# One large first load issued as three strided parts, ahead of the start barrier, in a kernel bound by data movement

## Chip, cores and metric

The kernel runs on one core of a Trainium2 chip. The metric is the time of one execution on the device in microseconds (us); lower is better. "The span" is the time from the first to the last instruction in a profile; it is 1.8 us shorter than the run's time.

## The reference

```python
def setup_inputs():
    batch, seq, dim = (32, 512, 2048)
    return {'x': np.random.randn(batch, seq, dim).astype(np.float32)}

def reference(x):
    half_dim = x.shape[-1] // 2
    x1, x2 = (x[..., :half_dim].copy(), x[..., half_dim:].copy())
    silu_x1 = x1 * (1 / (1 + np.exp(-x1)))
    return (silu_x1 * x2).astype(np.float32)
```

The input has 134.2 MB, the output 67.1 MB, and there is little arithmetic for each byte.

## The kernel before

Sixteen tiles of 1024 rows each; a partition holds 8 whole rows, 64 KB that lie together in memory. There are two input and two output buffers. ACT issues the loads and computes Silu in four chunks a tile, DVE multiplies, SP issues the stores.

```python
def issue_ahead_of_the_first_barrier(nc):
    head, body = nc.main_func.blocks[:2]
    load = next(ins for ins in body.instructions if type(ins).__name__ == "InstDMACopy")
    at = next(
        j for j, ins in enumerate(head.instructions)
        if ins.engine == load.engine and type(ins).__name__ == "InstDrain"
    )
    body.instructions = [ins for ins in body.instructions if ins.name != load.name]
    head.instructions = head.instructions[:at] + [load] + head.instructions[at:]
# ... (cut: sizes, pools, the plan of tiles)
    nc.at_finalize(issue_ahead_of_the_first_barrier)
    ctx.enter_context(tc.manual_schedule())
    loaded = {}

    def load(i):
        xt = in_pool.tile([P, K, in_cols], dt, name="xt")
        nc.scalar.dma_start(out=xt[:, :plan[i][1], :], in_=view(x_flat, i))
        loaded[i] = xt

    load(0)
    load(1)
    for i in range(n_tiles):
        # ... (cut)
        for c in range(0, k, KC):
            ce = min(c + KC, k)
            nc.scalar.activation(out=ot[:, c:ce, :], in_=xt[:, c:ce, :half],
                                 func=mybir.ActivationFunctionType.Silu)
            nc.vector.tensor_mul(out=ot[:, c:ce, :], in0=ot[:, c:ce, :],
                                 in1=xt[:, c:ce, half:])
            if last:
                nc.sync.dma_start(out=ov[:, c:ce, :], in_=ot[:, c:ce, :])
        if not last:
            nc.sync.dma_start(out=ov, in_=ot[:, :k, :])
        if i + 2 < n_tiles:
            load(i + 2)
```

The first load already stands ahead of the barrier with which the program starts, so that ACT's issue of it begins at 0.13 us of the span.

## Time and profile before

| | before |
|---|---|
| time, median of 3 runs | 470.96 us (470.91 to 471.08) |
| span of the profiled run | 468.9 us |
| busy: DVE, ACT | 30%, 25% |
| bytes moved | 201.35 MB, 429 GB/s on average |

The page of the kernel before: its span, the busy share of the engines, the busy tenths of the 16 DMA engines and the rate in 40 slices, and the chain of waits that ended last.

```profile
span 468.9 us, 269 instructions
DVE 142.3 (30%) x64; ACT 118.2 (25%) x65; POOL 0.2 (0%) x4
...
DMA  9899999999999998999999999999999989999998
GB/s 431 375 447 403 447 447 447 403 419 431 447 447 403 447 492 363 442 492 391 458 403 439 456 447 403 409 442 447 447 403 444 467 386 447 442 419 481 400 409 354
...
DMA 80%; DVE 15%; ACT 3%; DVEq 0%; issue 0%
```

The data movers hardly rest (the DMA row is 8 or 9 tenths in every slice); both compute engines idle most of the time (busy 30% and 25%). So in this kernel I expect a us in which the data movers do not move to come out as a us at the end.

The timeline of the kernel before, first 34 us: start, duration, engine (ACTq is ACT's sequencer, which issues DMAs), line, operation.

```profile
0.13 1.13 ACTq L74 DMA_DIRECT2D xt<-in_x_dram  x2
...
1.29 1.28 ACT L87 ACT_TABLE_LOAD   x1 [1.29 <-PEq L117]
21.88 7.31 ACT L87 ACTIVATE ot<-xt 128x2048 f32<-128x2048 f32 x4 [19.31 <-DMA xt<-in_x_dram]
23.82 8.90 DVE L92 TENSOR_TENSOR ot<-ot,xt 128x2048 f32<-128x2048 f32 x4 [23.82 <-ACT ot L87]
32.74 0.38 SPq L100 DMA_DIRECT2D out_dram<-ot  x1
32.75 0.35 ACTq L74 DMA_DIRECT2D xt<-in_x_dram  x1
```

ACT issues two loads, loads Silu's table while it waits, and starts on the first tile at 21.88 us. The first store is issued at 32.74 us.

The chain that ended last, in order of time (start, duration, what), beginning, second load and end:

```profile
0.92 43.60 DMA xt<-in_x_dram
...
55.41 47.19 DMA xt<-in_x_dram
...
404.13 46.88 DMA xt<-in_x_dram
...
451.03 1.92 ACT ot L87
```

The instructions on the input tile of the kernel before; the three numbers are the shortest, median and longest duration in ns of an issue on ACT.

```profile
L74 ACTq DMA_DIRECT2D xt<-in_x_dram x16: 334/366/376, 0.1 to 404.1; - x16
```

Below the page lie the records of single DMA packets. In this kernel one packet is one partition's row: 64 KB for a load, 32 KB for a store (8 KB for those of the last tile). The records do not name the engine; a figure "an engine" is a sum over all packets divided by 16. From them, with times from the start of the span:

```
kernel before                                     us
issue of the first load begins, ends              0.13, 0.50
first packets of the 16 engines begin             1.14 to 1.84, mean 1.32
first packets last                                2.47 to 3.44, on average 0.64 more than later ones
a load packet in mid-run lasts                    2.418   (27.1 GB/s an engine)
the load packet just ahead of an engine's first
store packet lasts                                3.18 to 3.42, on average 0.87 more than later ones
all load packets near the first store, longer by  0.90 an engine
last packet of all ends                           467.62
```

Each engine starts its next packet as the last one ends: between 5 and 450 us fewer than 16 of these packets are in flight for 1.0 us in all.

### The profile page before, as it was taken

To read this page: it belongs to the slowest core of one execution; us is meant where nothing else is said; L and a number is where in the kernel's file an instruction comes from. 1 tells how busy PE (TensorE), PEld (TensorE's weight loads), DVE (VectorE), ACT (ScalarE), POOL (GpSimd) and SP (SyncE) were. 2 spreads that over 40 slices of the span, in tenths; PEclk is the share of its full clock that TensorE was granted. 3 is DMA by queue.
4 is the path that set the end of the run, shared out by engine and by line. 5 is a ranking of instruction groups with operands and counts; after the bars stand their busy time and mean duration, and the time that the engine had idled before them with its cause. 6 is when DMAs were issued, how large, how long until landed. Compare 5 with 4: busy or idle time off the path is not lost.

```text
span 468.9 us, 269 instructions
## 1 busy us (share of the span) xinstructions
DVE 142.3 (30%) x64; ACT 118.2 (25%) x65; POOL 0.2 (0%) x4
## 2 busy tenths in 40 slices
DVE  0070705106061160601507025070250702407034
ACT  1142406023060330603206032060420604106051
POOL 0000000000000000000000000000000000000000
DMA  9899999999999998999999999999999989999998
GB/s 431 375 447 403 447 447 447 403 419 431 447 447 403 447 492 363 442 492 391 458 403 439 456 447 403 409 442 447 447 403 444 467 386 447 442 419 481 400 409 354
DMA packets 5042, 201.35 MB, mean 429 GB/s; under 512 B 560, under 2 KB 560, under 8 KB 560
## 3 DMA queue, kind: packets, MB, share of 16 engines
q10 hardware_dynamic: 2304, 134.22, 66.4%
q1 hardware_dynamic: 2736, 67.11, 33.2%
q14 instruction: 2, 0.02, 0.0%
HBM read 134.22 MB, written 67.11 MB: 429 GB/s over the span
## 4 chain that ended last, share of the span: by engine, by line
DMA 80%; DVE 15%; ACT 3%; DVEq 0%; issue 0%
DMA xt<-in_x_dram 80%; DVE ot L92 15%; ACT ot L87 3%; DVEq L128 0%
## 5 line engine op out<-in xcount | busy, mean ns | idle before, releaser
L92 DVE TENSOR_TENSOR ot<-ot,xt 128x2048 f32<-128x2048 f32 x64 | 142.3, 2286 | 319.5 <-ACT ot L87 319.5
L87 ACT ACTIVATE ot<-xt 128x2048 f32<-128x2048 f32 x64 | 116.9, 1897 | 338.8 <-DMA xt<-in_x_dram 338.8
L87 ACT ACT_TABLE_LOAD x1 | 1.3, 1283 | 1.3 <-PEq L117 1.3
L117 POOL MEMSET const-uint8-127<- 128x1 uint8 x1 | 0.1, 102 | 0.0
L117 POOL MEMSET const-bfloat16-1.0<- 128x1 bf16 x1 | 0.1, 101 | 0.0
L117 POOL MEMSET const-float32-0.0<- 128x1 f32 x1 | 0.1, 98 | 0.2 <-issue 0.2
L117 POOL MEMSET const-float32-1.0<- 128x1 f32 x1 | 0.1, 98 | 0.0
## 6 DMA issues: line engine op xcount, KB each, us to landing
out_dram<-ot SPq DMA_DIRECT2D x15, 4096.0 KB, 39.8
out_dram<-ot SPq DMA_DIRECT2D x4, 1024.0 KB, 5.7
xt<-in_x_dram ACTq DMA_DIRECT2D x16, 47.1
```

What stands on the lines that cost most here:

```text
L87: nc.scalar.activation(out=ot[:, c:ce, :], in_=xt[:, c:ce, :half], func=mybir.ActivationFunctionType.Silu,)
L92: nc.vector.tensor_mul(out=ot[:, c:ce, :], in0=ot[:, c:ce, :], in1=xt[:, c:ce, half:],)
L117: nc = _bacc.Bacc("TRN2", target_bir_lowering=False, num_devices=1)
```

## The change

The intent is that data starts to flow earlier after the issue of a first transfer with fewer rows. The first load is split into the partitions 0, 4, 8, ..., the ones halfway between (2, 6, 10, ...), and the odd ones, and all three parts are put ahead of the barrier.

```diff
-def issue_ahead_of_the_first_barrier(nc):
+def issue_ahead_of_the_first_barrier(nc, count):
     head, body = nc.main_func.blocks[:2]
-    load = next(ins for ins in body.instructions if type(ins).__name__ == "InstDMACopy")
+    loads = [ins for ins in body.instructions if type(ins).__name__ == "InstDMACopy"][:count]
     # ... (cut: all of `loads` are moved instead of one)
+    STARTING = [slice(0, None, 4), slice(2, None, 4), slice(1, None, 2)]
     # ... (cut)
-    nc.at_finalize(issue_ahead_of_the_first_barrier)
+    nc.at_finalize(lambda nc: issue_ahead_of_the_first_barrier(nc, len(STARTING)))
+    def load_parts(queue, dst, src, split):
+        for ps in STARTING if split else [slice(None)]:
+            queue.dma_start(out=dst[ps], in_=src[ps])
     def load(i):
         xt = in_pool.tile([P, K, in_cols], dt, name="xt")
-        nc.scalar.dma_start(out=xt[:, :plan[i][1], :], in_=view(x_flat, i))
+        load_parts(nc.scalar, xt, view(x_flat, i), split=i == 0)
     # ... (cut)
-            nc.sync.dma_start(out=ov, in_=ot[:, :k, :])
+            nc.sync.dma_start(out=ov, in_=ot)
```

The last line names the same region as before.

More of the change, by code (lines that the diff above doesn't have):

```diff
@@ L6 @@
 from concourse._compat import with_exitstack
-def issue_ahead_of_the_first_barrier(nc):
+def issue_ahead_of_the_first_barrier(nc, count):
     head, body = nc.main_func.blocks[:2]
-    load = next(ins for ins in body.instructions if type(ins).__name__ == "InstDMACopy")
+    loads = [ins for ins in body.instructions if type(ins).__name__ == "InstDMACopy"][:count]
     at = next(
         j for j, ins in enumerate(head.instructions)
-        if ins.engine == load.engine and type(ins).__name__ == "InstDrain"
+        if ins.engine == loads[0].engine and type(ins).__name__ == "InstDrain"
     )
-    body.instructions = [ins for ins in body.instructions if ins.name != load.name]
-    head.instructions = head.instructions[:at] + [load] + head.instructions[at:]
+    names = {ins.name for ins in loads}
+    body.instructions = [ins for ins in body.instructions if ins.name not in names]
+    head.instructions = head.instructions[:at] + loads + head.instructions[at:]
 @with_exitstack
```

## The prediction

> **What bounds the kernel.** Data movement, almost without a gap. The page's DMA row is 8 or 9 tenths in nearly every slice, mean 429 GB/s; DVE is busy 30%, ACT 25%. In the packet records a 64 KB load packet takes 2.418 us on its engine (27.1 GB/s), and each of 16 engines starts the next as the last ends. Every engine owes 128 load packets, 120 store packets of 32 KB (1.213 us) and 32 of 8 KB (0.309 us): 465 us. The first starts at 1.14 us of the span, the last ends at 467.6. What is not transfer is 1.3 us before the stream runs, some 0.6 us by which the first 16 packets are longer than later ones (2.5 to 3.4 us), and about 0.5 us at the end. The chain of waits agrees: 80% loads.
>
> **What the change does.** The first load, one issue of 128 rows of 64 KB, becomes issues of 32, 32 and 64 rows, all ahead of ACT's barrier drain. Bytes, row size, compute and its order stay (the store's changed slice is the same region).
>
> Added: two issues on ACT, 0.33 to 0.38 us each in the timeline. ACT's drain moves from 0.55 to about 1.2 us, the second load's issue from 0.92 to about 1.6 us. Neither is critical: the first part alone queues 4.8 us of work. Also 32 completion packets, two per engine at 9 ns: 0.02 us.
>
> Removed: some of the start. The issue runs from 0.13 to 0.50 us; engines begin between 1.14 and 1.39, two at 1.80 and 1.84. All finish their first packet together, at 4.24 to 4.60, whenever they began, as if data flowed only from about 1.85[...]. If a quarter as many descriptors make that sooner, the stream starts 0.1 to 0.5 us earlier and, saturated to its end, all of that comes off the time. If it is a first-access latency, nothing does. My estimate of the net: -0.3 us, 0.06%.
>
> **The risk.** [...] I give one in five to a loss of several us.
>
> **Predicted:** 470.7 us (before 470.96), range 470.0 to 473.0. Faster by over 2%: 0.01; within 2%: 0.86; slower by over 2%: 0.13.
>
> **What would show each step.** Timeline: three ACT issues, the last ending near 1.2 us; second load issued near 1.6. Packet records: earliest packet before 1.1 us, the first 16 closer together. The first ACTIVATE starts at 21.4 to 21.9 us (21.88 before); the last load lands 0.1 to 0.5 us before 451.0, as does the last store, 467.96. [...]
>
> **What would make it wrong.** [...] or engines idling between the parts.

The forecast's sum came to 470.96 - 0.3, about 470.7 us. The -0.3 is my estimate of the net: 0.1 to 0.5 us from an earlier start, or nothing, less 0.02 us for completion packets. The 4.8 us that the first part queues are an estimate too: two load packets of 2.418 us on each engine. The risk, that the strided parts of the first load would move more slowly: the one in five, the 0.13 for slower by over 2% and the upper part of the range, to 473.0 us, stood for it.

## The result

The changed kernel takes 471.94 us (median of 6 runs, 471.85 to 472.38) against 471.02 us (6 runs, 470.71 to 471.44): ratio 1.0021, 95% interval 1.0008 to 1.0033. By the 2% mark it is the same; the loss of about 0.9 us is nonetheless clear of the noise.

The page of the changed kernel, the same lines:

```profile
span 470.6 us, 274 instructions
...
DVE 142.4 (30%) x64; ACT 118.2 (25%) x65; POOL 0.2 (0%) x4
...
DMA  9999999999999999999999999999999999999997
GB/s 379 423 446 382 421 434 446 434 423 468 421 415 434 468 412 412 446 462 418 418 429 473 429 396 451 462 413 418 446 462 412 407 479 429 423 407 454 432 401 329
...
DMA 79%; DVE 15%; ACT 3%; DVEq 0%; issue 0%
```

At this grain nothing has changed: the bound is the same, and the page alone would not find 0.2%. The timeline does better. The changed kernel, first 36 us:

```profile
0.13 2.85 ACTq L76 DMA_DIRECT2D xt<-in_x_dram  x4
...
22.75 1.28 ACT L95 ACT_TABLE_LOAD   x1 [22.75 <-DMA xt<-in_x_dram]
24.05 7.31 ACT L95 ACTIVATE ot<-xt 128x2048 f32<-128x2048 f32 x4
25.99 8.90 DVE L100 TENSOR_TENSOR ot<-ot,xt 128x2048 f32<-128x2048 f32 x4 [25.99 <-ACT ot L95]
34.92 0.38 SPq L108 DMA_DIRECT2D out_dram<-ot  x1
34.92 0.35 ACTq L76 DMA_DIRECT2D xt<-in_x_dram  x1
```

Two things differ. The issues at the start last until 2.98 us (0.13 + 2.85) instead of 1.26. And the table load, 1.28 us, now comes after the load has landed: the first Silu waits for three transfers instead of one, and the trace has two of these waits on an extra instruction (a semaphore wait at 22.68 us) that stands ahead of the table load. So the first Silu starts 2.17 us later and the first store is issued 2.18 us later, though the load itself landed only 0.8 us later (22.66 against 21.86).

The chain, the same places:

```profile
2.64 43.34 DMA xt<-in_x_dram
...
56.87 47.10 DMA xt<-in_x_dram
...
405.53 47.09 DMA xt<-in_x_dram
...
452.64 1.92 ACT ot L95
```

The loss is there after the second load, which lands at 45.97 us instead of 44.52, and does not grow much afterwards: 1.45 us at the second load, 1.61 at the last. So what happens before 46 us is all there is to explain.

The issues on the input tile:

```profile
L76 ACTq DMA_DIRECT2D xt<-in_x_dram x18: 348/366/615, 0.1 to 405.5; - x18
```

The longest issue is 615 ns. The three strided ones last 0.550, 0.602 and 0.615 us; no load issue of the kernel before lasts over 0.376. And in the packet records, for this profile and for a second one of the same kernel (run "after_again" below):

```
                                          before  changed  changed again
first packet of any engine begins           1.14     1.47     1.46
first packets begin, mean                   1.32     1.75     1.60
first packets longer by, mean               0.64     0.58     0.68
load packets longer at the first store,
  us an engine                              0.90     1.50     1.50
engines on which such a packet starts
  before 37.5 us / long packets in all     16/16     4/20     7/23
second load: last engine done after first   0.38     2.30     2.16
last packet of all ends                   467.62   469.25   468.47
```

The sum for the first pair: 0.43 us from the later start, -0.06 from the first packets, 0.60 from the packets at the first store; that leaves 0.66 of the 1.63 us for what the slowest engine lags behind the mean more than it did before. For the second profile: 0.28 + 0.04 + 0.60 = 0.92 of 0.85, the lag being a little smaller than before. The start was in the prediction, with the wrong sign. The first store was not in it at all.

### The profile page after: what moved, and what is told of

Its sections match the earlier page's. It is cut to its first block, busy times and chain, and to the rows that moved or that the text cites. A ratio compares the mean times of both kernels' runs of the same rounds, so it can differ in the third digit from the quotient of the medians.

```text
span 470.6 us, 274 instructions
## 1 busy us (share of the span) xinstructions
DVE 142.4 (30%) x64; ACT 118.2 (25%) x65; POOL 0.2 (0%) x4
## 4 chain that ended last, share of the span: by engine, by line
DMA 79%; DVE 15%; ACT 3%; DVEq 0%; issue 0%
DMA xt<-in_x_dram 79%; DVE ot L100 15%; ACT ot L95 3%; DVEq L136 0%
```

## The experiments

Two theories, which can both be true.

- Theory S: the strided issues make the stream start later, and as it is saturated, the end comes as much later.
- Theory P: the later first store meets the 16 engines while some of them pass a packet boundary before it reaches them and some after. Some take up the store one load packet earlier than the others. The lengthening at the first store is then 1.4 to 1.5 us an engine instead of 0.9, and the engines stay out of step.

Every run was correct, and in 5 rounds unless said.

### after_again: does the trace repeat?

No edit; the changed kernel once more.

> The changed kernel once more, to see which parts of its trace repeat. Theory S (the start): three issues of 0.55 to 0.62 us each and engines that begin 0.33 us later or more cost what the stream loses, since it is saturated to its end: the first 16 packets end on average 0.4 us later than before, every time, and the whole is 0.9 us (0.2%) slower. Theory P (the phase at the first store): of the 1.7 us between the two profiled spans, 0.6 us comes from load packets that are 0.9 us longer (before) or 1.2 us longer on average (after) when the first store begins at 36 to 41 us; four engines switch to the store one packet earlier than the other twelve and end up to 1.4 us later. If P is a steady part of the loss, four or so engines lag again here; if it was chance of that one profile, they do not.

Measured: 471.70 us (471.62 to 471.90) against 471.02, ratio 1.0015 (1.0001 to 1.0028). The later start is there (0.28 us in the mean), the 1.50 us at the first store are there, and the engines split again, 7 to 9. What does not repeat is the 1.4 us by which the last engines trailed in the first profile, which was also the slowest of its six runs. The steady loss is 0.7 to 0.9 us.

### table_early: the first store 1.5 us earlier, the start untouched

```diff
     load(0)
     load(1)
+    first_ot = out_pool.tile([P, K, half], dt, name="ot")
+    nc.vector.memset(first_ot[:, 0, 0:1], 0.0)
+    nc.scalar.activation(out=first_ot[:, 0, 0:1], in_=first_ot[:, 0, 0:1],
+                         func=mybir.ActivationFunctionType.Silu)
     # ... (cut: the first tile's ot is this first_ot)
```

> The changed kernel, with the ACT table load pulled ahead of the wait for the load by one 128x1 Silu. Theory S: the table load is not on the path that matters (the data movers are busy meanwhile); time as the changed kernel's within 0.1 us, 471.9. Theory P: the first store is issued 1.3 us earlier (33.6 instead of 34.9), meets the load packets at another place of their 2.42 us cycle, and the time moves by up to 0.6 us, in either direction. A third reading, that a later first tile simply delays everything: 1.3 us faster.

The timeline of this run:

```profile
3.02 1.28 ACT L89 ACT_TABLE_LOAD   x1 [3.02 <-PEq L132]
...
22.56 7.31 ACT L102 ACTIVATE ot<-xt 128x2048 f32<-128x2048 f32 x4 [18.05 <-DMA xt<-in_x_dram]
...
33.42 0.37 SPq L115 DMA_DIRECT2D out_dram<-ot  x1
```

Measured: 471.43 us (471.18 to 471.76), ratio to before 1.0009 (0.9997 to 1.0022). The start is as late as in the changed kernel (mean 1.67), but the lengthening at the first store is back at 0.94 us, on all 16 engines at the same boundary, and the second load's engines finish within 0.81 us. The store came 1.5 us earlier than in the changed kernel and the time fell by only 0.3 to 0.5, so a later first tile does not simply delay everything. What remains over the kernel before, 0.4 us by the medians, is what theory S asks for.

### store_late, store_mid, store_later: the start of before, the first store moved

The kernel before with one useless Silu ahead of the first tile's work, of 2385, 1502 or 3208 elements a partition (the real Silu overwrites its result):

```diff
+        if i == 0:   (the two slices set the length; here store_late)
+            nc.scalar.activation(out=ot[:, 2:5, :795], in_=xt[:, 2:5, :795],
+                                 func=mybir.ActivationFunctionType.Silu)
         for c in range(0, k, KC):
```

> The kernel before, with one useless Silu ahead of the first tile's work that holds up its store by about 2.2 us, as in the changed kernel; the start is untouched. Theory S: no loss, 471.0. Theory P: part of the loss of the changed kernel shows up, 0.3 to 0.6 us, with the lengthened packets near 38 us. If a later first tile delays everything: 2.2 us slower, 473.2.

> The same with a shorter useless Silu, first store issued near 34.2 us. Theory P: the boundaries near 35.8 us fall 1.4 to 1.8 us after the issue, inside the window in which the store reaches the engines, so they split: lengthening 1.3 to 1.5 us, time 471.4 to 471.6. Rival, lateness: between the kernel before and store_late, 471.2 to 471.3.

> The kernel before with the useless Silu made longer, so that the first store is issued near 35.7 us, later than in any run so far (store_late: 34.97). Theory P, sharpened: a store reaches an engine 1.0 to 1.7 us after its issue and is taken up at that engine's next packet boundary; boundaries here lie near 33.4, 35.8 and 38.2 us, 2.42 apart. When all 16 engines take it up at the same boundary the lengthening is 0.9 us an engine, when they are split over two it is 1.4 to 1.5. At 35.7 all take it up at 38.2: lengthening 0.9 us, time as before, 471.0, although the store is later than in store_late (471.56). Rival, lateness itself: 471.6 or more and a lengthening of 1.4 us or more.

The timeline of store_late, whose first store is issued at the changed kernel's moment after an untouched start:

```profile
0.13 1.14 ACTq L74 DMA_DIRECT2D xt<-in_x_dram  x2
...
22.03 2.19 ACT L86 ACTIVATE ot<-xt 128x2385 f32<-128x2385 f32 x1 [19.44 <-DMA xt<-in_x_dram]
...
34.97 0.37 SPq L106 DMA_DIRECT2D out_dram<-ot  x1
```

Ordered by the moment of the first store, with the packet records beside the times ("split" counts the engines that lengthen a packet before 37.5 us, that is at the earlier boundary):

| run | first store issued, us | split of 16 | long packets in all | longer, us an engine | second load, first to last engine, us | time, us | ratio to before |
|---|---|---|---|---|---|---|---|
| before | 32.7 | 16 | 16 | 0.90 | 0.38 | 471.02 | 1 |
| store_mid | 34.4 | 1 | 17 | 1.25 | 2.84 | 471.74 (471.03 to 472.87) | 1.0012 (0.9999 to 1.0026) |
| store_late | 35.0 | 2 | 18 | 1.39 | 3.13 | 471.56 (470.98 to 471.97) | 1.0009 (0.9996 to 1.0021) |
| store_later | 35.7 | 0 | 16 | 1.19 | 0.74 | 471.03 (470.85 to 471.79) | 0.9996 (0.9983 to 1.0008) |

The medians of before that go with the four rows are 471.02, 471.25, 471.02 and 471.25 us. The latest store has no cost that these runs can show, and the two in the middle cost about 0.5 us. So it is not lateness; the split is what the two have in common. When one or two engines take up the store a packet ahead of the rest, each of them has two long packets (the long packets in all are 16 plus the early engines), the rest pay more than 0.9, and at the end of the second load the early engines are 2 to 3 us behind the first. Of these, 1.2 us is the store packet that they have moved already (1.213 us in before); the rest is lag. Theory P missed in sizes: with the store at 35.7 the lengthening was to be 0.9 us and was 1.19, while the split was indeed gone. In store_mid it expected more engines on the early side than the one that there was, and a lengthening of 1.3 to 1.5 where 1.25 was measured. So a part of the extra lengthening, 0.2 to 0.3 us, comes with the later boundary and not with the split. The intervals of the single ratios hold 1. Taken together, the ten runs of store_mid and store_late are 0.5 us slower in the mean than the 18 runs of before from their rounds, give or take 0.4 (two standard errors); store_later is 0.15 us faster, give or take 0.4.

Why these moments: the first load's packets begin 1.0 to 1.7 us after its issue (0.13 to 1.14 and 1.84), and not on all engines at once. If a store takes as long to reach the engines, those that pass a boundary inside such a window after its issue fall on both sides. In the kernel before, boundaries lie at 33.2 to 33.6 and 35.7 to 36.0 us; a store issued at 32.74 is too late for the first and in time for the second on every engine. The packet records of the runs bear this out for stores. A boundary here is the start of the load packet that comes just ahead of an engine's first store packet, or could have. In before, table_early, store_later, after_late, in_body, rows_cut, warm_write and two_queues, which are not split, the boundaries up to 0.85 us after the store's issue were all missed and those from 2.3 us on were all met. In the changed kernel, after_again, store_mid and store_late, boundaries 1.1 to 1.9 us after the issue went either way. The strided start also spreads the boundaries themselves, over 35.8 to 36.9 us instead of 35.7 to 36.0; that this is why more engines split in the changed kernel (4 and 7) than in store_mid and store_late (1 and 2) is likely, not tested.

Do the early engines stay behind to the end? In the changed kernel 4 engines stop after 468.6 us, the others by 468.3; in store_mid it is 1 (468.70, the others by 467.9), in store_late 3 (468.46 to 468.94, the others by 467.7). That is close to the 4, 1 and 2 early engines. But the records do not name them, after_again with its 7 has no such clear gap, and table_early, which is not split, has a straggler too (468.61, the others by 468.0). The lag of the last engine behind the mean is 0.3 to 1.3 us from profile to profile (rows_cut 0.1), so one profile's end is no measure of a few tenths.

### after_late: the changed kernel with its first store later still

The same useless Silu, 1444 elements, in the changed kernel.

> The changed kernel with a useless Silu of about 1.4 us ahead of the first tile's work, so that its first store is issued near 36.1 us, later still than its 34.9. Theory P: the engines' packet boundaries lie at 35.8 to 36.9 and 38.2 to 39.3 us; at 36.1 nearly all take the store up at 38.2 or later, unsplit: lengthening 1.0 to 1.2 us instead of 1.5, and the time falls to 471.3 to 471.5, that of table_early, although the store is later. If lateness costs: over 472.

Measured: first store issued at 35.80 us, no engine on the early side, lengthening 1.11 us, second load within 0.76 us. 471.56 us (471.11 to 471.60), ratio 1.0007 (0.9994 to 1.0020), a little above the 471.3 to 471.5 expected. Adding work did not slow the changed kernel down; against its 471.70 and 471.94 it was, if anything, faster. It stays above before by about what the start costs. Taken together, the ten runs of table_early and after_late are 0.4 us slower in the mean than the 18 runs of before from their rounds, give or take 0.2 (two standard errors); the eleven of the changed kernel are 0.8 slower than their 15, give or take 0.2. So about half of the loss goes with the split, and this difference is clear of the noise.

### in_body: the start later, nothing else

```diff
-    nc.at_finalize(issue_ahead_of_the_first_barrier)
```

> The kernel before, with its first load left behind the barrier, issued near 0.85 us instead of 0.13. Theory S: every us by which the stream starts later is a us at the end: first packets 0.7 to 0.8 us later, the first store's issue as well and with it its place against the packet boundaries, so the lengthening stays 0.9 us and the time is 0.7 to 0.8 us longer, 471.7 to 471.8. If there were slack after the start, less.

Measured: the issue begins at 0.73 us instead of 0.13, the first packets 0.61 us later in the mean, lengthening 0.86 us, last packet 0.75 us later than in the profile of before. Time 471.67 us (471.41 to 472.17) against 471.25, ratio 1.0008 (0.9995 to 1.0020). The profile agrees with a start that is passed on in full; the timed difference, 0.4 us, is smaller than expected, and its interval holds both 0 and 0.7.

### contiguous: stride or count, and the rate

```diff
-    STARTING = [slice(0, None, 4), slice(2, None, 4), slice(1, None, 2)]
+    STARTING = [slice(0, 32), slice(32, 64), slice(64, 128)]
```

> The changed kernel with contiguous parts: partitions 0 to 31, 32 to 63, 64 to 127. Theory: it is the count of rows and issues, not the stride, that makes the issues long (0.55 to 0.62 us instead of 0.38): the issues stay as long and the start as late. Rival: the stride makes them long: 0.33 to 0.38 us here and a start near 1.1 us. [...]

The rate in this run, from 2 us on in stretches of 10 us; the last number is GB/s:

```profile
2.00:12.00 10.00, 0.00 (x0) 0.00 (x0) 0.00 (x0) 1.00 1.05 216
12.00:22.00 10.00, 0.00 (x0) 0.00 (x0) 0.00 (x0) 1.00 1.01 210
22.00:32.00 10.00, 0.00 (x0) 0.00 (x0) 0.00 (x0) 1.00 0.96 197
```

Measured (4 runs): 490.94 us (490.85 to 491.13), ratio 1.0422 (1.0408 to 1.0437). The three issues last 0.383, 0.437 and 0.529 us, and the first packet begins at 1.14 us. So the stride, not the count of rows, makes the first issue long (0.550) and the first packet 0.33 us late. And 32 rows start no sooner than 128: the first packet begins at 1.14 us in both. The change's premise fails there.

For as long as the first load runs, the rate is half: 216 to 197 GB/s in these stretches, against 419 in each of them in the kernel before. A packet lasts 5.12 us instead of 2.418, in spite of 16 busy engines (the busy share in the stretches is 1.05 to 0.96); 16 packets of 64 KB in 5.12 us are 205 GB/s. What limits these parts, no run here shows. In the changed kernel the strided parts run at 2.418 us a packet, so of the two splits by partitions only the strided one keeps the rate.

### rows_cut: three issues without a stride

```diff
-    STARTING = [slice(0, None, 4), slice(2, None, 4), slice(1, None, 2)]
+    STARTING = [slice(0, 2), slice(2, 4), slice(4, 8)]
-            queue.dma_start(out=dst[ps], in_=src[ps])
+            queue.dma_start(out=dst[:, ks], in_=src[:, ks])
     (and the early table load of table_early)
```

> The first load in three issues of all 128 partitions, cut along the rows (16, 16 and 32 KB of each), with the early table load. Theory S, that the stride and not the number of issues makes the start late: issues of 0.33 to 0.45 us, first packet near 1.14 us and mean start 1.3 to 1.45, time 470.9 to 471.2, as before. If three issues ahead of the barrier are what costs: mean start 1.6 or more and 471.4 or more.

Measured: the start is that of before (issues 0.376, 0.449, 0.453 us; first packet 1.14, mean 1.28), no split, lengthening 0.94 us, and still 471.98 us (471.87 to 472.15), ratio 1.0019 (1.0005 to 1.0033). The expectation of the time failed, though that of the start held. The reason is at the other end. Windows of rows_cut, and then of before (the last two numbers are the DMA engines' busy share and GB/s):

```profile
456.00:459.00 3.00, 3.00 (x2) 3.00 (x3) 0.00 (x0) 1.00 0.48 205
```

```profile
456.00:459.00 3.00, 3.00 (x2) 2.34 (x2) 0.00 (x0) 1.00 0.84 355
```

In rows_cut the first tile's chunks are computed as their parts land and the first store is issued at 28.43 us, 4.3 us earlier than before. The packet records show no active engine at all between 457.80 and 458.56 us, and the last load lands at 453.4 us instead of 451.0. My reading is that stores which run further ahead of the loads leave less of a backlog to move while the last tile is computed; the empty stretch is seen, the link to the early first store was not tested by itself.

### warm_write, two_queues, store_act: what is the lengthening at the first store?

```diff
 warm_write (before):
+    nc.sync.dma_start(out=view(out_flat, 0)[:, 0, 0:128], in_=view(x_flat, 0)[:, 0, 0:128])
     (put ahead of the barrier as well; the first store overwrites it)
 two_queues (before, and the early table load):
-        nc.scalar.dma_start(out=xt[:, :plan[i][1], :], in_=view(x_flat, i))
+        nc.sync.dma_start(out=xt[:, :4, :], in_=src[:, :4, :])
+        nc.scalar.dma_start(out=xt[:, 4:, :], in_=src[:, 4:, :])
     (both ahead of the barrier)
 store_act (before):
-            nc.sync.dma_start(out=ov, in_=ot[:, :k, :])
+            (nc.scalar if i == 0 else nc.sync).dma_start(out=ov, in_=ot[:, :k, :])
```

> The kernel before with one small copy put ahead of the barrier on the other DMA queue: 512 bytes of each of 128 rows from the input to the output, which the first store overwrites later. It makes each engine write to the output while the stream is still starting. If the 0.9 us lengthening at the first store is a cost of an engine's first write to the output, it is gone from 36 us and shows, if at all, in the first packets; where it overlaps the start, the time falls to 470.2 to 470.5. If it is a cost of mixing the two queues for the first time with full-size packets, it stays at 36 us and the time is 471.0 to 471.2.

> The first load in two halves of its rows, one issued on each DMA queue ahead of the barrier, with the early table load. If the lengthening at the first store is paid whenever two queues first share the engines, it is paid at the start here, partly under the start's own delay, and there is none at the first store: down to 470.2 to 470.7. If it belongs to the first store, or comes whenever a second queue joins, it stays near 0.9 us and the time is 470.9 to 471.2. SP's issue may begin at 0.00 instead of 0.13, which would give at most 0.1 us.

> The kernel before with its first store on the queue of the loads, so it runs after the second load and in one ring with it. If the lengthening comes from two queues sharing the engines, it is gone from 36 us and comes up when the second store joins on the other queue, near 58 us. If it comes from the first writing beside reading, it is seen where the first store's packets run, near 44 us. In either case I expect the time within 0.5 us of before.

Measured:

| run | time, us | before, same rounds | ratio | longer at the first store, us an engine |
|---|---|---|---|---|
| warm_write | 471.16 (470.98 to 471.42) | 471.25 | 0.9997 (0.9984 to 1.0009) | 0.84, near 36 us |
| two_queues | 470.75 (470.65 to 470.96) | 470.98 | 0.9993 (0.9980 to 1.0005) | 0.96, near 36 us |
| store_act | 471.17 (471.08 to 472.26) | 470.98 | 1.0009 (0.9996 to 1.0021) | 1.13, near 38 us |

A small early write to the output does not take it away, nor does having had both queues at work with packets of 32 KB from the start. In store_act, where the first store runs behind the second load on the same queue, it is again the load packet just ahead of the first store packet that is longer (the last of the second load, from 38.0 us), and when the second store joins on the other queue, issued at 53.3 us, only six load packets grow, by less than 0.16 us each. So in these runs it goes with the first large store, on whichever queue, once on each engine (twice on the early engines of a split). In all runs but contiguous it is 0.84 to 0.96 us an engine when all 16 meet it at the boundary near 36 us (near 31 us in rows_cut), 1.11 to 1.19 one packet later, and 1.25 to 1.50 when they are split over two. One run does not fit: in contiguous, whose first store is issued only at 55.5 us, no load packet after the first load lasts over 2.43 us, although the engines split there too (14 take up the store at 59.1 to 59.4 us, 2 a load packet later). So the lengthening is not bound to every first store, nor to every split. What the engines do in that time stays open.

two_queues has the lowest median of all runs; its first packets begin 0.13 us earlier in the mean. The interval holds 1, so I do not call it faster, and no version here beats the kernel before.

## Why the prediction was right in its range and wrong in its sign

- **The bound** was read rightly: the chain and the DMA rows stay the same in the changed kernel, and the time stays within 0.2%. The range of 470.0 to 473.0 us held 471.94, but that was luck as far as the start is concerned: its upper part stood there for a slower first load, which did not come, and the loss that filled it has other causes. Of the marks that the prediction set for the gain none came true: the last early issue ends at 1.96 us (1.2 forecast), the second load is issued at 2.64 (1.6), the first packet begins at 1.47 (before 1.1), the first Silu starts at 24.05 (21.4 to 21.9), and the last load lands at 452.62 (0.1 to 0.5 before 451.0).
- **The gain at the start**, "the stream starts 0.1 to 0.5 us earlier", is the step that failed. The first packets begin 0.28 to 0.43 us later in the mean. In the kernel before the first packet begins 1.0 us after its issue begins and 0.63 us after it ends (0.13, 0.50, 1.14); in the changed kernel it begins 0.79 us after the end of the first strided issue (0.68, 1.47). Contiguous parts show that 32 rows start no sooner than 128 (1.14 us both), and that the stride makes the first issue 0.17 us longer and the first packet 0.33 us later. The other branch that the prediction named, a first-access latency, fits better: first packets are 0.6 to 0.75 us longer in the mean in every run but contiguous, whose packets were slow throughout the first load (5.12 us), whatever was issued. That it is a latency is not shown; that the change does not shorten it is.
- **The added issues**, "0.33 to 0.38 us each", were mis-sized: 0.550, 0.602 and 0.615. That the later ones would not be critical was right; the engines did not run dry between the parts (from 2.46 us, when 16 packets are in flight, to 30 us there are fewer for 0.11 us in all).
- **What was left out.** The prediction followed the issues on ACT but not the waits of the first Silu. Three transfers mean three waits, and two of them came to stand ahead of the table load and put its 1.28 us behind the load. That moved the first store by 2.18 us, into the moment at which the engines split. table_early and after_late take the split away with the start left as it is, and about half of the loss goes with it; store_mid and store_late put it into the kernel before with its start as it is, and about the same half comes up. So the loss of 0.7 to 0.9 us is, by the times, about 0.4 us of start and 0.4 to 0.5 us of the first store's moment. By the packet records it is 0.3 to 0.4 us of start and 0.6 us of longer packets, beside a lag at the end that differs between profiles.
- **The risk** of a slower first load did not come true: the strided packets keep 2.418 us. The contiguous parts show that the choice of partitions can cost as much: packets of 5.12 us, and 20 us in all (490.94 against 471.02). The prediction's reasons for the risk are not shown by these runs.

## What to carry to other kernels

Splitting a transfer also multiplies the waits of its reader (here three for one): look at which instruction these waits now stand on, and whether something that used to be hidden has moved behind them, as the table load of 1.28 us did here. In this stream, which moves data from start to end, 0.4 to 0.5 us were lost where the engines fell out of step (store_mid, store_late), about as much as the 0.1 to 0.5 us that the change was to gain. So compare the packet records at each place where the traffic changes (start, first store, end), not only at the place that was edited. And before building on "fewer rows start sooner", run the smallest such transfer alone and read when its first packet begins; here 32 and 128 rows both began at 1.14 us.
